# The sums of squares of the second half of x, taken up from the tenth projection step on instead of the fifth

## The chip, the core and the metric

The kernel runs on one core of one Trainium2 chip. The metric is the device time of one execution in microseconds, as the median of several runs. A core has TensorE (PE in the rows, its weight loads PEld), VectorE (DVE), ScalarE (ACT), GpSimd (POOL) and SyncE (SP), which here issues the DMAs. Each engine works through its own queue of instructions in the order in which the program wrote it, and waits at semaphores for the others.

## What is computed

One layer of a decoder: sliding-window attention with sinks, between a projection of the normalised input and a projection of the gated output. x has 2048 tokens of 2048 features, all in float32. There are 32 query heads and 4 key and value heads of 64 features each; a block of 128 queries sees its own and the block of keys before it.

```python
h = rms_norm(x, swa_norm)                        # mean of x*x over the features
q, k, v, gate = split(h @ w_in)                  # 2048, 256, 256, 2048 columns
q, k = rms_norm(q, q_gain), rms_norm(k, k_gain)  # by head
s = q @ k * 64 ** -0.5 + bias[distance]          # 128 queries x 256 keys, banded
m = max(max(s), sink)
p = exp(s - m) / (sum(exp(s - m)) + exp(sink - m))
out = x + ((p @ v) * silu(gate)) @ w_out
```

The part that the change touches is the mean of x*x over the features, of which there is one number for each token. It enters the key and query norms as a small correction (eps_t) and scales the values and gates (rstd).

## The kernel before

**Tiling.** The tokens are worked on in two halves of 1024 (HALF). For each half the transposed x lies in SBUF as 16 tiles, each split into a high and a low part (bigh, bigl), and a projection step takes 128 columns of w_in: three matmuls (L148, L151, L154) for each of the 16 tiles and of two column groups of 512 tokens, so 96 matmuls into the two accumulators acc. There are 40 such steps, numbered from 0: for each half and each of two pairs of key heads a step for the keys, one for the values and eight for the queries. Steps 0 to 9 and 10 to 19 are the two pairs of the first half, 20 to 29 and 30 to 39 those of the second.

**Attention units.** Beside the matmuls of step n the program emits attention units (beside, unit) whose queries are ready: four units for each query step, 128 in all, each with two blocks of queries and two heads. A unit has scores s (8 matmuls, L329; written 4 and 4 where it is the first block), a masking copy on VectorE (L333, L334, L337), the reading of the scores with scale and bias into lg (L342, 4 instructions), maximum and exponentials (L346 to L357), normalisation on GpSimd (L360), four transposes (pt, L364), copies and masks, eight output matmuls (o, L383; 6 for a first block), and a store. In PSUM there is one buffer each for s, pt and o; lg has two.

**The statistics.** For the first half the squares are summed while x is loaded. For the second half block_sums (L170) does it: for each of eight blocks of 128 tokens it loads four pieces of x in its untransposed form (xb, L174) and squares each on ScalarE with an accumulator (L175). Then stats(1) (L177) reduces the 32 columns to one number for each token, forms eps_t and rstd, and transposes rstd on PE (tp, L191) through the o buffer and an lg buffer (rr, L192, L193), writes it to DRAM (r_sp, L194) and reads it back as a row (rb, L198), which the gates use much later. The squares' buffers come from the pool evp (4 buffers), which the key and value work and the query squares use as well.

**The loop.** Lines 492 to 506 run over the steps from 3 on: load the next weights, block_sums of one block in steps 4 to 11, stats(1) in step 12, the units, the 96 matmuls, and the work on the result (evacuate). Ahead of step 20 the second half of x is loaded (load_big(1), L100 to L102). After the 40 steps come the gates and the output projection (from L507 on), 14 passes of 8 steps with 48 matmuls each.

**What sets the order.** The program is given to a scheduler, which simulates it and writes the instructions of every engine in the order in which its simulation could start them, by the order of emission as a priority; key work and the loading of x stand higher than their place. So an emission that moves changes the written order of every engine around it, and later, and the matmuls of units and projections interleave in another way.

Of the kernel before, what the change touches and what calls it, by code (L numbers as in the profile page):

```python
# [21 lines left out]
NB = HALF // P  # L22
# [9 lines left out]
def swa_layer_kernel(ctx: ExitStack, tc: tile.TileContext, xT: bass.AP, x: bass.AP, w_in: bass.AP,  # L32
# [60 lines left out]
    def load_big(c, ks=range(KT), cuts=(0, HALF), xsq=None):  # L93
        hi, lo = [], []
        for k in ks:
            raw = st.tile([P, HALF], F32, tag="raw", name="raw", bufs=RAW)
            h, l = [big.tile([P, HALF], F32R, tag="big", name=n) if k < KT - 2 else
                    rest.tile([P, HALF], F32R, tag="rest", name=n) for n in ("bigh", "bigl")]
            for a, b in zip(cuts, cuts[1:]):
                nc.sync.dma_start(out=raw[:, a:b], in_=xT[k * P:(k + 1) * P, c * HALF + a:c * HALF + b])  # L100
                nc.scalar.activation(out=h[:, a:b], in_=raw[:, a:b], func=AF.Copy, scale=gT[:, k:k + 1])  # L101
                nc.vector.scalar_tensor_tensor(out=l[:, a:b], in0=raw[:, a:b], scalar=gT[:, k:k + 1],  # L102
                                               in1=h[:, a:b].bitcast(F32), op0=ALU.mult, op1=ALU.subtract)
                if xsq:
                    square_sums(k, raw, a, b, xsq)
            hi.append(h)
            lo.append(l)
        return hi, lo


    def load_stat(src, qs=range(2), cuts=(0, HALF), between=None, eng=nc.vector):
        parts = []
        for q in qs:
            raw = st.tile([P, HALF], F32, tag="raw", name="raw", bufs=RAW)
            for a, b in zip(cuts, cuts[1:]):
                nc.sync.dma_start(out=raw[:, a:b].rearrange("p (k c) -> p k c", c=P),
                                  in_=src[:, q * 8 + a // P:q * 8 + b // P, :])
                if between and a == 0:
                    between()
            parts += split_stat(raw, cuts, eng)  # L120
        return parts
# [19 lines left out]
    def gemm(stat, res, acc=None, ks=range(KT), last=KT - 1):  # L141
        if acc is None:
            acc = new_acc()
        for k in ks:
            h, l = stat[k // 4]
            cs = slice((k % 4) * P, (k % 4 + 1) * P)
            for n in range(2):
                nc.tensor.matmul(acc[n], h[:, cs], res[0][k][:, n * CH:(n + 1) * CH],  # L148
                                 start=(k == 0), stop=False)
            for n in range(2):  # L150
                nc.tensor.matmul(acc[n], h[:, cs], res[1][k][:, n * CH:(n + 1) * CH],  # L151
                                 start=False, stop=False)
            for n in range(2):
                nc.tensor.matmul(acc[n], l[:, cs], res[0][k][:, n * CH:(n + 1) * CH],  # L154
                                 start=False, stop=(k == last))
        return acc
# [13 lines left out]
    def block_sums(b):  # L170

        for i in range(4):
            xs = evp.tile([P, CH], F32, tag="ev", name="xb")
            nc.sync.dma_start(out=xs, in_=x[b * P:(b + 1) * P, i * CH:(i + 1) * CH])  # L174
            nc.scalar.activation(out=xs, in_=xs, func=AF.Square, accum_out=msum[:, b % NB, i:i + 1])  # L175

    def stats(c, xsq=None):  # L177
        bs = slice(c * NB, (c + 1) * NB)
        ms = at.tile([P, NB], F32, tag="ms", name="ms")
        if xsq:  # L180
            ss = ps_t.tile([P, NB], F32, tag="t", name="xss")
            for b in range(NB):
                nc.tensor.matmul(ss[:, b:b + 1], xsq[b // 4][:, b % 4 * P:(b % 4 + 1) * P], ones, start=True, stop=True)
        else:
            ss = at.tile([P, NB], F32, tag="xss", name="xss", bufs=1)
            nc.vector.tensor_reduce(out=ss, in_=msum, op=ALU.add, axis=AX.X)
        nc.vector.tensor_scalar(out=ms, in0=ss, scalar1=1.0 / D, scalar2=EPS, op0=ALU.mult, op1=ALU.add)
        nc.vector.tensor_scalar(out=eps_t[:, bs], in0=ms, scalar1=EPS, scalar2=None, op0=ALU.mult)
        nc.gpsimd.tensor_tensor(out=rstd[:, bs], in0=ms, in1=mhalf[:, 0:NB], op=ALU.pow)
        tp = ps_o.tile([P, CH], F32, tag="o", name="tp")  # L190
        nc.tensor.transpose(out=tp[0:NB, 0:P], in_=rstd[:, bs], identity=ident)  # L191
        rr = at.tile([P, CH], F32, tag="lg", name="rr")  # L192
        nc.vector.tensor_copy(out=rr[0:NB, 0:P], in_=tp[0:NB, 0:P])  # L193
        nc.sync.dma_start(out=r_sp[c][:, :], in_=rr[0:NB, 0:P])  # L194
# [205 lines left out]
    def stat_src(step):  # L400
        kind, c, i = step
        return w_in[{"q": 0, "k": 16, "v": 18}[kind] + i]
# [7 lines left out]
    def evacuate(step, acc, copies=None):  # L410
        kind, c, i = step
        if kind == "q":
            queries[i, c] = evac_q(acc, c)
        elif kind == "k":
            with tc.high_priority(offset=400):
                evac_k(acc, c, i, copies or copy_out(acc))
        else:
            evac_v(acc, c, i, copies or copy_out(acc))
# [3 lines left out]
    def beside(n):  # L422

        for cb, j in units.get(n, []):
            c, half = j // NB, j % NB // 4
            if (cb, c) not in bias:
                bias[cb, c] = load_bias(cb)
            if (cb // 4, c, half) not in kv:
                kv[cb // 4, c, half] = load_kv(cb // 4, c, half)
            qs, rq = queries[cb, c]  # L430
            unit(cb, j, qs[half], rq, *kv[cb // 4, c, half], bias[cb, c])
# [60 lines left out]
    for n, step in enumerate(steps):  # L492
        if n < 3:
            continue
        nxt = load_stat(stat_src(steps[n + 1]), eng=nc.gpsimd) if n + 1 < len(steps) else None
        if 4 <= n < 4 + NB:
            block_sums(NB + n - 4)
        elif n == 4 + NB:
            stats(1)
        beside(n)  # L500
        acc = gemm(stat, res)
        if n + 1 < len(steps) and steps[n + 1][1] != step[1]:
            with tc.high_priority(offset=300):
                res = load_big(1)
        evacuate(step, acc)
        stat = nxt
# [269 lines left out]
```

## Time and profile before

| | |
|---|---|
| median of 3 runs | 2465.68 us (2463.45 to 2465.91) |
| the profiled execution | 2466.36 us |
| its span | 2464.6 us |
| mean granted clock of PE | 0.994 |
| PE busy | 2431.2 us, 99% of the span |
| VectorE, GpSimd, ScalarE busy | 67%, 44%, 39% |

The span is the time from the first to the last instruction, and the execution's own time lies 1.8 us above it. The profile is one execution. Its views that are used here: the busy time by engine; the busy time in stretches of 20 us with the granted clock as a share of the full 2.4 GHz; the table of who waited for whom; the chain of waits, which follows the end of the work back to what released each piece; the rows of one tile; and the timeline of an engine. Counted off in PE's projection matmuls in the trace, 96 to a step, step 8 lies at 210 to 251 us, steps 10 and 11 at 280 to 355, step 14 at 414 to 439, step 19 at 560 to 590, steps 20 and 21 at 590 to 666, and step 31 at 931 to 964.

### The profile page before, as it was taken

The numbers are of one execution on the slowest core, as the hardware profiler recorded it, in microseconds if no ns is written. First come the engines' busy times: TensorE is split into PE (matmuls) and PEld (weight loads), VectorE is DVE, ScalarE is ACT, GpSimd is POOL, SyncE is SP. The second block draws the span as 40 slices with busy tenths as digits, with TensorE's granted clock in tenths as the row PEclk, the third lists the DMA queues.
The fourth block names the chain that finished last, engine by engine and source line by source line (L and its number), as shares of the span: only waits on it lengthen the run. The fifth ranks groups of instructions, "written<-read, shape, count | busy, mean of one in ns | idle before, by whom it ended". The sixth has DMA issues, their size and how long they took to land.

```text
span 2464.6 us, 35291 instructions
## 1 busy us (share of the span) xinstructions
PE 2431.2 (99%) x11858; PEld 2044.4 (83%) x11858; DVE 1648.4 (67%) x3206; ACT 971.6 (39%) x2387; POOL 1092.3 (44%) x1041
## 2 busy tenths in 40 slices
PE   8999999999999999999999999999999999999999
PEld 7888888887788888888887888888888888888887
DVE  7287777789777877887864776576684436554533
ACT  7255545456545545554543332222232212122110
POOL 0156666575656666666541343034451033113434
PEclk9999999999999999999999999999999999999999
DMA  7322333125331223212127997687887679678755
GB/s 228 104 95 90 109 98 119 59 68 172 107 105 57 78 63 105 86 52 84 65 86 269 316 363 257 236 271 260 263 271 260 224 228 346 213 265 278 262 181 175
DMA packets 211380, 429.39 MB, mean 174 GB/s; under 512 B 20208, under 2 KB 91520, under 8 KB 211200
## 3 DMA queue, kind: packets, MB, share of 16 engines
q1 hardware_dynamic: 211200, 427.15, 53.1%
q8 instruction: 94, 1.54, 0.3%
q14 instruction: 86, 0.70, 0.1%
HBM read 336.88 MB, written 90.19 MB: 173 GB/s over the span
## 4 chain that ended last, share of the span: by engine, by line
PE 87%; DMA 7%; DVE 3%; POOL 1%; issue 1%; ACT 1%; SPq 0%; DVEq 0%; POOLq 0%; ACTq 0%
PE acc L148 25%; PE acc L151 25%; PE acc L154 25%; PE s L329 5%; PE o L383 5%; DMA braw<-xT 2%; PE pt L364 2%; DMA out<-craw 1%; DMA craw<-x 1%; DMA raw<-xT 1%; DVE parts L520 0%; DMA braw<-t_sp 0%; POOL craw L523 0%; DVE braw L520 0%; DVE braw L572 0%
## 5 line engine op out<-in xcount | busy, mean ns | idle before, releaser
L148 PE MATMUL acc<-bigh,wh 128*128 128x512 f32 x1472 | 494.4, 396 | 7.7 <-ACT bigh L101 5.5
L154 PE MATMUL acc<-bigh,wl 128*128 128x512 f32 x1472 | 491.1, 394 | 0.0
L151 PE MATMUL acc<-bigl,wh 128*128 128x512 f32 x1472 | 490.5, 395 | 0.1
L523 POOL TENSOR_TENSOR craw<-craw,u 128x512 f32<-128x512 f32 x112 | 163.0, 1469 | 419.7 <-DMA craw<-x 229.1
L148 PEld LDWEIGHTS acc<-bigh,wh 128*128 128x128 f32 x1472 | 274.3, 190 | 58.3 <-ACT bigh L101 5.5
L151 PEld LDWEIGHTS acc<-bigl,wh 128*128 128x128 f32 x1472 | 275.2, 190 | 51.9 <-DVE bigl L102 1.3
L154 PEld LDWEIGHTS acc<-bigh,wl 128*128 128x128 f32 x1472 | 274.5, 190 | 50.5
L355 ACT ACTIVATE lg<-lg,nm 128x128 f32<-128x128 f32 x512 | 199.9, 392 | 185.0 <-DVE nm L348 169.2
L151 PE MATMUL acc<-obl,parts 128*128 128x512 f32 x768 | 236.6, 389 | 1.4 <-DVE obl L520 1.4
L154 PE MATMUL acc<-obh,parts 128*128 128x512 f32 x768 | 236.6, 389 | 0.4 <-DVE parts L520 0.4
L154 PE MATMUL acc<-obh,wl 128*128 128x512 f32 x768 | 236.5, 389 | 0.0
L148 PE MATMUL acc<-obh,parts 128*128 128x512 f32 x768 | 236.4, 389 | 0.0
L148 PE MATMUL acc<-obh,wh 128*128 128x512 f32 x768 | 236.4, 389 | 0.0
L151 PE MATMUL acc<-obl,wh 128*128 128x512 f32 x768 | 236.4, 389 | 0.0
L134 POOL TENSOR_TENSOR wl<-raw,wh 128x512 fp32r<-128x512 f32 x144 | 187.5, 1303 | 94.7 <-ACT wh L133 87.9
L523 POOL TENSOR_TENSOR araw<-araw 128x1024 f32<-128x1024 f32 x48 | 119.6, 2492 | 225.5 <-DMA araw<-o_sp 75.3
L360 POOL TENSOR_TENSOR lg<-lg,den 128x512 f32<-128x512 f32 x128 | 134.1, 1048 | 112.1 <-DVE den L359 74.0
L563 ACT CAST obh<-braw 128x1024 fp32r<-128x1024 f32 x80 | 83.9, 1053 | 230.1 <-DVE braw L520 108.7
L151 PEld LDWEIGHTS acc<-obl,parts 128*128 128x128 f32 x768 | 143.9, 188 | 31.8 <-DVE obl L520 2.2
L154 PEld LDWEIGHTS acc<-obh,parts 128*128 128x128 f32 x768 | 144.2, 188 | 30.9 <-DVE parts L520 0.9
L151 PEld LDWEIGHTS acc<-obl,wh 128*128 128x128 f32 x768 | 144.2, 188 | 30.0
L148 PEld LDWEIGHTS acc<-obh,parts 128*128 128x128 f32 x768 | 144.1, 188 | 30.1
(136 smaller groups left out, 4405.8 us busy)
## 6 DMA issues: line engine op xcount, KB each, us to landing
braw<-w_out SPq DMA_DIRECT2D x88, 512.0 KB, 5.6
araw<-w_in SPq DMA_DIRECT2D x80, 512.0 KB, 5.7
araw<-o_sp SPq DMA_DIRECT2D x80, 512.0 KB, 5.7
raw<-w_in SPq DMA_DIRECT2D x79, 512.0 KB, 3.7
braw<-xT SPq DMA_DIRECT2D x72, 512.0 KB, 5.8
craw<-o_sp SPq DMA_DIRECT2D x80, 256.0 KB, 4.9
o_sp<-og SPq DMA_DIRECT2D x128, 128.0 KB, 1.9
o_sp<-craw SPq DMA_DIRECT2D x64, 256.0 KB, 5.0
```

Source lines behind the costliest of these rows:

```text
L134: eng.tensor_tensor(out=l[:, a:b], in0=r, in1=h[:, a:b].bitcast(F32), op=ALU.subtract)
L148: nc.tensor.matmul(acc[n], h[:, cs], res[0][k][:, n * CH:(n + 1) * CH], start=(k == 0), stop=False)
L151: nc.tensor.matmul(acc[n], h[:, cs], res[1][k][:, n * CH:(n + 1) * CH], start=False, stop=False)
L154: nc.tensor.matmul(acc[n], l[:, cs], res[0][k][:, n * CH:(n + 1) * CH], start=False, stop=(k == last))
L329: nc.tensor.matmul(s[:, b, h, lo:], qq[:, h, (i0 + b) * P:(i0 + b + 1) * P], kk[:, i, (i0 + b) * P + lo:(i0 + b + 2) * P], start=(i == 0), ...
L355: nc.scalar.activation(out=lg[:, b, h], in_=lg[:, b, h], func=AF.Exp, bias=nm[:, b, h:h + 1], accum_out=den[:, b, h:h + 1])
L360: nc.gpsimd.tensor_tensor(out=lf, in0=lf, in1=den.rearrange("p b h -> p (b h)").unsqueeze(2).broadcast_to([P, 4, P]), op=ALU.mult)
L364: nc.tensor.transpose(out=t[:, i, :], in_=lf[:, i, :], identity=ident)
L383: nc.tensor.matmul(o[:, 2 * b:2 * b + 2, :], v, p[:, 2 * b:2 * b + 2, :], start=(i == 0), stop=(i == len(terms) - 1))
L523: nc.gpsimd.tensor_tensor(out=out, in0=a, in1=b, op=op)
L563: nc.scalar.copy(out=h, in_=src)
```

## The change

The block sums move from steps 4 to 11 to steps 9 to 16, and stats(1) from step 12 to step 17. Each step still takes one block, in the same order of blocks.

```diff
@@ -493,9 +493,9 @@
         if n < 3:
             continue
         nxt = load_stat(stat_src(steps[n + 1]), eng=nc.gpsimd) if n + 1 < len(steps) else None
-        if 4 <= n < 4 + NB:
-            block_sums(NB + n - 4)
-        elif n == 4 + NB:
+        if 9 <= n < 9 + NB:
+            block_sums(n - 9 + NB)
+        elif n == 9 + NB:
             stats(1)
         beside(n)
         acc = gemm(stat, res)
```

What the scheduler makes of it, at three places. In these rows a name is a tile, and what stands behind the arrow is read. The names: acc are the projections, s the scores, pt the transposes, o the outputs of attention units.

PE's queue in step 8 before, from the second group of scores (a first block) on; ahead of these rows stand a score group, four transposes and six outputs.

```order
L329 MATMUL s<-kk,qq 128x256 x4
L364 MATMUL pt<-ident,lg 128x128 x4
L383 MATMUL o<-php,vv 128x256
L383 MATMUL o<-plp,vv 128x256
L383 MATMUL o<-ph,vv 128x256
L383 MATMUL o<-pl,vv 128x256
L383 MATMUL o<-php,vv 128x256
L383 MATMUL o<-plp,vv 128x256
L383 MATMUL o<-ph,vv 128x256
L383 MATMUL o<-pl,vv 128x256
L329 MATMUL s<-kk,qq 128x256 x8
L148 MATMUL acc<-bigh,wh 128x512
```

The same place after.

```order
L329 MATMUL s<-kk,qq 128x256 x4
L364 MATMUL pt<-ident,lg 128x128 x4
L383 MATMUL o<-php,vv 128x256
L383 MATMUL o<-plp,vv 128x256
L383 MATMUL o<-ph,vv 128x256
L383 MATMUL o<-pl,vv 128x256
L383 MATMUL o<-php,vv 128x256
L383 MATMUL o<-plp,vv 128x256
L383 MATMUL o<-ph,vv 128x256
L383 MATMUL o<-pl,vv 128x256
L148 MATMUL acc<-bigh,wh 128x512
L151 MATMUL acc<-bigl,wh 128x512
```

The third score group has moved away from behind the eight outputs; it now follows after 21 projection matmuls.

PE's queue in step 15 before, behind the row transpose tp. Between tp and these rows stand 23 projection matmuls.

```order
L148 MATMUL acc<-bigh,wh 128x512 x2
L151 MATMUL acc<-bigl,wh 128x512
L329 MATMUL s<-kk,qq 128x256 x8
L151 MATMUL acc<-bigl,wh 128x512
L154 MATMUL acc<-bigh,wl 128x512 x2
L148 MATMUL acc<-bigh,wh 128x512 x2
L151 MATMUL acc<-bigl,wh 128x512 x2
L154 MATMUL acc<-bigh,wl 128x512 x2
L148 MATMUL acc<-bigh,wh 128x512 x2
L151 MATMUL acc<-bigl,wh 128x512 x2
L154 MATMUL acc<-bigh,wl 128x512
L364 MATMUL pt<-ident,lg 128x128 x4
```

PE's queue after, behind tp, which now stands in step 19. Between tp and these rows stand 14 projection matmuls.

```order
L148 MATMUL acc<-bigh,wh 128x512
L151 MATMUL acc<-bigl,wh 128x512
L154 MATMUL acc<-bigh,wl 128x512
L329 MATMUL s<-kk,qq 128x256 x8
L364 MATMUL pt<-ident,lg 128x128 x4
L329 MATMUL s<-kk,qq 128x128 x4
L329 MATMUL s<-kk,qq 128x256 x4
L383 MATMUL o<-php,vv 128x256
L148 MATMUL acc<-bigh,wh 128x512
L151 MATMUL acc<-bigl,wh 128x512
```

From tp to the first transposes pt it was 40 projection matmuls and a score group, and is 17 and a score group; a second score group follows those transposes at once.

SyncE's queue around the write of the transposed row before: w_in are weights, og outputs of units.

```order
L390 DMA o_sp_102<-og 128x256
L116 DMA raw<-w_in 128x1024
L194 DMA r_sp_152<-rr 8x128
L198 DMA rb_15243<-r_sp_152 128x1024
L116 DMA raw<-w_in 128x1024
L390 DMA o_sp_103<-og 128x256
L305 DMA bias<-band 128x256
L116 DMA raw<-w_in 128x1024
```

SyncE's queue there after: xT is the second half of x, kk and vv are keys and values.

```order
L100 DMA raw<-xT 128x1024
L316 DMA vv<-v_sp_94 128x4x128
L390 DMA o_sp_106<-og 128x256
L194 DMA r_sp_152<-rr 8x128
L198 DMA rb_15243<-r_sp_152 128x1024
L315 DMA kk<-k_sp_90 128x2x640
L305 DMA bias<-band 128x256
L100 DMA raw<-xT 128x1024 x2
L390 DMA o_sp_106<-og 128x256
L100 DMA raw<-xT 128x1024 x5
```

The write (L194) and the read (L198) stood among loads of weights, and now stand behind the first of the 16 loads of x and ahead of the other 15.

PE's queue in step 31 before, around the transposes of the second pair's keys (L247).

```order
L148 MATMUL acc<-bigh,wh 128x512
L151 MATMUL acc<-bigl,wh 128x512
L154 MATMUL acc<-bigh,wl 128x512
L247 MATMUL acc<-ident,kv 128x128 x8
L148 MATMUL acc<-bigh,wh 128x512
L151 MATMUL acc<-bigl,wh 128x512
L154 MATMUL acc<-bigh,wl 128x512
L148 MATMUL acc<-bigh,wh 128x512
L151 MATMUL acc<-bigl,wh 128x512
L154 MATMUL acc<-bigh,wl 128x512
L148 MATMUL acc<-bigh,wh 128x512
L364 MATMUL pt<-ident,lg 128x128
```

PE's queue in step 31 after, some way ahead of those transposes. A score group, four transposes and eight outputs stand just ahead of these rows.

```order
L329 MATMUL s<-kk,qq 128x256 x8
L364 MATMUL pt<-ident,lg 128x128 x4
L383 MATMUL o<-php,vv 128x256
L383 MATMUL o<-plp,vv 128x256
L383 MATMUL o<-ph,vv 128x256
L383 MATMUL o<-pl,vv 128x256
L383 MATMUL o<-php,vv 128x256
L383 MATMUL o<-plp,vv 128x256
L383 MATMUL o<-ph,vv 128x256
L383 MATMUL o<-pl,vv 128x256
L329 MATMUL s<-kk,qq 128x256 x8
L148 MATMUL acc<-bigh,wh 128x512
```

Three score groups now stand with only transposes and outputs between them, where before projection matmuls stood. In steps 10 and 11 PE's queue has the same rows before and after, and ScalarE's squares stand in the same places.

## Rows read from the trace of the kernel before

**Rows 1.** The page's busy time of each engine, us (share of the span) xinstructions.

```profile
PE 2431.2 (99%) x11858; PEld 2044.4 (83%) x11858; DVE 1648.4 (67%) x3206; ACT 971.6 (39%) x2387; POOL 1092.3 (44%) x1041
```

**Rows 2.** Stretches: length, busy PE, PEld, DVE, ACT, POOL, clock, DMA share, GB/s.

```profile
220.00:240.00 20.00, 16.52 (x86) 14.16 (x85) 17.08 (x50) 12.76 (x44) 10.65 (x14) 0.83 0.34 106
...
280.00:300.00 20.00, 18.17 (x101) 15.79 (x100) 17.08 (x46) 10.97 (x37) 9.94 (x16) 0.91 0.23 71
...
320.00:340.00 20.00, 18.67 (x102) 15.66 (x101) 16.72 (x42) 13.45 (x45) 10.45 (x15) 1.00 0.26 83
340.00:360.00 20.00, 18.30 (x98) 15.70 (x97) 14.84 (x40) 9.19 (x31) 15.30 (x13) 0.91 0.35 98
...
420.00:440.00 20.00, 20.00 (x94) 16.60 (x93) 8.83 (x28) 5.05 (x15) 9.31 (x9) 1.00 0.27 87
...
580.00:600.00 20.00, 18.40 (x90) 14.09 (x90) 18.84 (x31) 13.59 (x26) 11.22 (x10) 1.00 0.68 202
600.00:620.00 20.00, 17.52 (x85) 14.22 (x84) 19.66 (x39) 12.69 (x23) 10.36 (x10) 0.92 0.60 196
620.00:640.00 20.00, 17.84 (x98) 15.29 (x97) 16.92 (x42) 11.25 (x38) 13.14 (x16) 0.99 0.32 107
640.00:660.00 20.00, 20.00 (x102) 16.89 (x102) 15.48 (x47) 10.72 (x38) 13.57 (x12) 0.91 0.17 47
660.00:680.00 20.00, 18.12 (x107) 15.29 (x106) 12.10 (x32) 9.79 (x26) 12.01 (x16) 1.00 0.66 171
...
960.00:980.00 20.00, 20.00 (x121) 17.75 (x120) 15.24 (x41) 12.53 (x41) 13.04 (x17) 1.00 0.73 204
```

**Rows 3.** PE's waits, 100 to 700 us: us in total, times, longest.

```profile
PE s L329 <- DVE lg L342: 5.8, 5, 2.2
PE pt L364 <- DVE pl L368: 2.7, 3, 1.9
PE o L383 <- POOL plp L372: 1.9, 3, 1.3
```

**Rows 4.** The tile xb of the squares: duration ns min/median/max, first and last start.

```profile
L174 SPq DMA_DIRECT2D xb<-x x32: 328/336/1438, 126.6 to 368.3; - x32
L175 ACT ACTIVATE xb<-xb x32: 614/631/638, 130.4 to 376.0; 128x512 f32<-128x512 f32 x32
L175 ACT ACTIVATION_READ_ACCUMULATOR xb<-xb x32: 184/188/197, 131.0 to 376.5; 128x1 f32 x32
```

**Rows 5.** The chain of waits, 205 to 235 us: start us, us, what.

```profile
220.96 0.95 PE s L329 x8
...
222.34 0.72 PE o L383 x6
...
229.33 1.14 DVE lg L342 x4
...
230.60 2.04 PE s L329 x8
```

**Rows 6.** Timeline of DVE and POOL behind the row transpose: start us, us, instruction.

```profile
435.07 0.28 DVE L193 COPY rr<-tp 8x128 f32<-8x128 f32 x1 [4.52 <-PE tp L191]
435.28 1.10 DVE L342 SCALAR_TENSOR_TENSOR lg<-s,rq,bias 128x128 f32<-128x128 f32 x4
...
439.64 1.04 POOL L360 TENSOR_TENSOR lg<-lg,den 128x512 f32<-128x512 f32 x1 [4.67 <-ACT wh L133]
```

**Rows 7.** Timeline of PE at the row transpose.

```profile
434.76 0.27 PE L191 MATMUL tp<-ident,rstd 128*8 128x128 f32 x1
...
435.10 0.63 PE L151 MATMUL acc<-bigl,wh 128*128 128x512 f32 x2
435.57 0.61 PE L154 MATMUL acc<-bigh,wl 128*128 128x512 f32 x2
```

**Rows 8.** Timeline of SyncE's queue there: issue us, us.

```profile
435.42 0.29 SPq L194 DMA_DIRECT2D r_sp<-rr  x1
438.73 0.34 SPq L198 DMA_DIRECT2D rb<-r_sp  x1
```

## The prediction

> **What bounds the kernel now.** I read the page's busy line first [rows 1]: TensorE (PE) is busy for 2431.2 of 2464.6 us. So only what makes PE stand, or run at a lower clock, can move the time; what other engines do counts where PE waits for it. Next come the 20 us stretches of the first 1320 us [rows 2]. I use one measure throughout: the loss of a stretch is 20 us less PE's busy time, plus 20 us times what the granted clock lacks to 1.00 (part of such a stretch ran at the 1.2 GHz level in place of 2.4). Four of the stretches shown lie in the first half of x: 220:240 loses 3.48 + 3.4 = 6.9 us, 280:300 1.83 + 1.8 = 3.6, 320:340 1.3, 340:360 1.7 + 1.8 = 3.5; together 15.3. Five lie around the loading of the second half, 580 to 680: 1.6 + 4.1 + 2.4 + 1.8 + 1.9 = 11.7. The stretches 420:440 and 960:980 lose nothing; they hold the row transpose of the statistics and the key and value steps of the second half's second pair.
>
> What is waited for there: the table of PE's waits from 100 to 700 us has as its largest row scores (s, L329) behind the reading of the scores before them (lg, L342), 5.8 us in 5 waits [rows 3]. There is one buffer of scores, so the scores of a unit can't start before VectorE has read those of the unit ahead. Where projection matmuls (acc) stand between two score groups, that costs nothing. The chain of waits through 220 to 232 us shows the other case [rows 5]: scores at 220.96, outputs (o) to 223.06, then six or seven microseconds in which ScalarE and VectorE lead the chain, the reading of scores at 229.33, the next scores at 230.60. PE follows its written order, so the projections queued behind do not fill this. I call such a place, with score groups separated only by transposes and outputs of other units, a knot.
>
> The sums of squares themselves: 32 loads, issued from 126.6 to 368.3 us, and 32 squares with 32 accumulator reads on ScalarE, 0.631 + 0.188 = 0.82 us each, 26.2 us in all [rows 4]. They are on PE's path nowhere directly: no row of PE's waits names them among its largest.
>
> **The change part by part.** *The sums.* Nothing is removed or added: the same 32 loads, 32 squares, one reduction, one transpose, two small DMAs. The 26.2 us of ScalarE go from steps 5 to 12 into steps 10 to 17. By themselves I cost this at nothing: what hides it is ScalarE's idle time, since it is busy for 39% of the span [rows 1]. Where a square delays an exponential or a cast on PE's path it costs up to 0.82 us; in steps 10 and 11, where PE's order stays, ScalarE has squares in the same places before and after. What the move does is make the scheduler place everything else differently, and there the sum lies.
>
> *Step 8's knot.* Before, three score groups stand with only transposes and outputs between; now the third has 21 projection matmuls ahead of it. What is left is the pattern that stands in step 10, before and after alike, and step 10 loses 3.6 us (280:300). So 6.9 becomes 3.6: a gain of **3.3 us**; bounds 0 (the loss is of the remaining pair) and 6.9 (all goes).
>
> *Steps 10 and 11.* PE's order is the same row for row, so 3.6 + 1.3 + 3.5 us stay: 0.
>
> *Step 31's new knot.* Here the new order has three score groups in a row, with 4 transposes and 8 outputs between each, ahead of the transposes of the second pair's keys. The old order had projections there and 960:980 lost nothing. The nearest row is step 8's old knot, 6.9 us: the same three groups with the same transposes, outputs and query casts between, and no square beside them that I would have to take off. The bounds are 0 (VectorE is less busy here) and 8 (that knot with a wait more). I take **+6.9 us**.
>
> *The row transpose of the statistics (tp, L191).* It moves from step 14 to step 19. The pass behind it is measured: transpose at 434.76, copy (L193) at 435.07, reading of the next scores at 435.28, normalised exponentials (L360) at 439.64 + 1.04 = 440.68 us [rows 6, 7]; so 5.9 us from transpose to the next unit's transposes. Before, 40 projection matmuls and a score group cover that. Now 17 projections at 0.23 us (two take 0.47 from start to start [rows 7]) and one score group of 0.95 [rows 5] cover 3.9 + 0.95 = 4.9: a wait of 1.0 us. Behind it the next scores come at once, and wait for a masking copy, a query cast and the reading (0.7 + 0.7 + 1.1 us by the same kind of rows; of these only the reading, 1.14, is in rows 5): I take 1.2 us. The first output then waits some 0.4 us. That is **+2.6 us**; bounds 0, and 4.3 with one fall of the clock as in 280:300 or 340:360 (1.8).
>
> *Steps 20 to 22.* The units that stood still around the transpose are caught up here. Now there are three places where a score group follows the one before with 1.1 to 1.4 us of PE work between; before there was one, with 0.6. But the VectorE work between the query casts of step 17 and the key work of step 20 is the same in both orders (12 units and the 16 loads of x), and this stage was held by VectorE and the loads. I keep 11.7 us, so **0**; bounds -3 (the loads stand closer together) and +8 (two of the places at step 10's 3.6, and a little).
>
> Sum: -3.3 + 0 + 6.9 + 2.6 + 0 = +6.2 us. The profiled execution took 2466.36 us with a span of 2464.6; the median is 2465.68, so the profile stands for the runs within 0.7 us, and I add the sum to the median: 2465.7 + 6.2 = **2471.9 us**, 0.25% slower. A measurement of this kernel can tell about 0.2% (4.9 us) from no change.
>
> **The rivals.** *No change that can be measured.* Step 31's knot costs half or less (3 us), since VectorE there has no x to take up: -3.3 + 3 + 2.6 = +2.3, 2468 us. For it: 960:980 lost nothing. Against: no three groups stood in a row there.
>
> *Faster.* The mechanism is step 8: 6.9 us go entirely if it was the squares on ScalarE, four of them in a row of that knot, that held the query casts and through them VectorE; then step 31, without squares, costs nothing, and 2465.7 - 6.9 = 2458.8, or 2461.4 with the transpose's 2.6. It decides at the point where a knot without squares costs under 1 us. Against it: in ScalarE's order the squares stand behind the exponentials of the knot's first two units, and 280:300 lost 3.6. The Trainium skill, Perfetto Trace Analysis, Optimization Strategy, says that a gap that repeats on the engine that should be saturated can mean too few buffers for the next tile; by that the single score buffer sets the loss and squares do not, the largest row of PE's waits agrees, and a gain by the squares would not come.
>
> *The loads of x held up, slower still.* On the queue of SyncE the write of r_sp and the read of rb now stand ahead of 15 of the 16 loads of the second half of x; before, they stood among loads of weights. In the trace the read went 3.31 us after the write was issued (435.42 to 438.73) [rows 8], and nothing was issued between. If this falls where the loads are what PE waits for, 3.3 us more and a fall of the clock (1.8) come on top: 2471.9 + 5.1 = 2477 us. Against it: step 19 now begins with 36 projections with hardly anything between, which frees the old x sooner. The Trainium skill, DMA: Bandwidth & Descriptors, Anatomy of one DMA, says that a wait for a semaphore happens on the issuing sequencer before dispatch; by that the wait for the landed row keeps all loads behind it back, and the trace agrees in the 3.31 us, which is this rival's price.
>
> That the sums come too late for their reader, the second half's first keys, is excluded: the reduction stands at step 17 and VectorE has it ahead of those keys in either order.
>
> **How the numbers follow.** The forecast has a chance of 0.38, the held loads 0.12, no change 0.33, faster 0.17. Slower by over 0.2% (above 2470.6): 0.38 + 0.12 = 0.50; within: 0.33; faster (below 2460.8): 0.17. The range reaches from 2460, a little under the faster case with the transpose's cost, to 2482, the held loads with the upper bound of one further place (+5); below and above I leave 0.1 each.
>
> **What would show it.** In the profile after, the stretch around 220 us should lose about 3.6 us, that around 285 and 345 as before; a new loss of 6 to 7 us should stand near 930 to 950, with scores behind the reading of scores as PE's waits; a loss of 2 to 4 near 565; 580 to 680 about 12. I am wrong if 900 to 960 stays without loss, or if 580 to 680 loses under 8 or over 17 us: then the stage of the loads, which I put at zero, decided.

## The result and the profile after

The changed kernel takes 2486.83 us (median of 5 runs, 2484.04 to 2494.16), the kernel before beside it 2464.41 us: a ratio of 1.0094, with an interval of 1.0077 to 1.011. It is slower, as forecast, but by 22 us and not by 6, and outside the range. The profiled execution took 2486.83 us too, with a span of 2485.1.

The page's busy line of the changed kernel answers [rows 1]: the instructions of every engine are as many as before, so the 20.5 us of span are waits and clock. PE's busy time rose by 6.0 us with the same 11858 matmuls, with a granted clock of 0.91 in 560 to 680 us in place of 0.97; the other 14.5 us are PE standing.

```profile
PE 2437.2 (98%) x11858; PEld 2045.3 (82%) x11858; DVE 1649.0 (66%) x3206; ACT 973.5 (39%) x2387; POOL 1098.6 (44%) x1041
```

The stretches of the changed kernel answer [rows 2], with the same columns (length; busy PE, PEld, DVE, ACT, POOL; clock, DMA share, GB/s).

```profile
220.00:240.00 20.00, 18.18 (x100) 15.59 (x99) 17.63 (x47) 10.48 (x34) 11.46 (x14) 0.91 0.25 80
...
280.00:300.00 20.00, 17.78 (x104) 15.24 (x103) 16.95 (x45) 11.97 (x41) 10.80 (x17) 1.00 0.30 96
...
320.00:340.00 20.00, 18.65 (x112) 15.96 (x111) 17.79 (x50) 14.78 (x47) 10.83 (x12) 1.00 0.34 100
340.00:360.00 20.00, 18.24 (x97) 15.36 (x96) 11.81 (x29) 8.13 (x26) 15.11 (x17) 1.00 0.49 126
...
540.00:560.00 20.00, 20.00 (x99) 16.78 (x98) 2.98 (x7) 3.63 (x6) 8.33 (x11) 1.00 0.26 85
560.00:580.00 20.00, 17.91 (x95) 14.95 (x94) 16.57 (x40) 8.02 (x25) 7.10 (x8) 1.00 0.34 95
580.00:600.00 20.00, 15.40 (x68) 12.02 (x68) 18.09 (x35) 15.19 (x33) 12.62 (x10) 0.83 0.48 163
600.00:620.00 20.00, 15.85 (x68) 11.71 (x69) 19.79 (x31) 13.04 (x22) 9.62 (x10) 0.83 0.70 226
...
940.00:960.00 20.00, 17.11 (x98) 14.14 (x97) 14.34 (x38) 9.66 (x33) 9.65 (x16) 1.00 0.08 27
```

By the prediction's measure of loss, and from rows like these, the difference between 200 and 2440 us is made up so:

| us from the start | loss before | loss after | difference |
|---|---|---|---|
| 200 to 280 | 6.7 | 3.9 | -2.8 |
| 280 to 360 | 8.1 | 5.3 | -2.8 |
| 360 to 540 | 0.1 | 2.4 | +2.3 |
| 560 to 680 | 11.7 | 26.6 | +14.9 |
| 900 to 1000 | 0.0 | 4.1 | +4.1 |
| 1360 to 1460 | 0.4 | 4.8 | +4.4 |
| all other | 8.5 | 7.3 | -1.2 |

The sum is +18.9; the other 1.6 us of the 20.5 lie below what this measure sees. Most of the unexpected time stands in 560 to 680, where the second half of x is loaded. These two rows show that stretch as one, before and then after, and are the yardstick for the experiments (loss: 120 - 111.89 + 3.6 = 11.7, and 120 - 104.23 + 10.8 = 26.6).

```profile
560.00:680.00 120.00, 111.89 (x584) 92.85 (x583) 101.32 (x230) 70.19 (x177) 74.78 (x76) 0.97 0.46 139
```

```profile
560.00:680.00 120.00, 104.23 (x519) 85.81 (x518) 104.94 (x236) 69.20 (x181) 69.87 (x68) 0.91 0.40 128
```

**What the trace shows there.** The row of 540 to 560 is the odd one: VectorE is busy for 2.98 of 20 us, right ahead of the stage of the loads, in which it is busy for 18 to 20 of 20 us from 580 to 640. Its timeline in the changed kernel shows three waits in a row, the last of them for the row transpose (in brackets: idle before, and what ended it).

```profile
547.28 0.69 DVE L368 TENSOR_TENSOR pl<-pt,ph 128x512 fp32r<-128x512 f32 x1 [6.55 <-ACT ph L366]
547.89 0.84 DVE L389 TENSOR_TENSOR og<-o,bot 64x256 f32<-64x256 f32 x2
555.56 0.85 DVE L389 TENSOR_TENSOR og<-o,bot 64x256 f32<-64x256 f32 x2 [6.83 <-ACT bot L386]
560.93 0.28 DVE L193 COPY rr<-tp 8x128 f32<-8x128 f32 x1 [4.52 <-PE tp L191]
561.14 1.10 DVE L342 SCALAR_TENSOR_TENSOR lg<-s,rq,bias 128x128 f32<-128x128 f32 x4
```

PE lost nothing meanwhile: it ran projections. What it left out are attention units, which stand behind the transpose. VectorE's reading of scores ahead of the copy began at 530.22, so it takes up no new unit for 30 us. The next reading stands right behind the row's copy in VectorE's queue, and starts ahead of the row's write (561.24): what holds it is this place in the written order, and not the write. In the table of VectorE's waits in the kernel before, the same last wait stood ahead of step 14's transpose, with the same 4.5 us: there too VectorE stood half idle, 8.83 of 20 us in the row 420:440 of [rows 2]. So the hole in VectorE's work was there before. What is new is where it lies.

Behind it, the chain of waits of the changed kernel (start, us, what) runs through VectorE and the loads, PE hardly appearing: readings of scores and query casts of the late units stand between the low parts of x (bigl), and the low parts release the buffer of the next load.

```profile
589.00 0.69 DVE qq L214
...
589.72 1.13 DVE lg L342 x4
...
592.04 1.27 DVE bigl L102
...
593.32 3.73 DMA raw<-xT
...
597.08 1.07 ACT bigh L101
...
599.16 0.60 DVE lg L342 x2
599.76 0.73 DVE bigl L102
```

The waits of SyncE's queue, 500 to 700 us, give the same from the side of the loads (us in total, times, longest): before, then after.

```profile
SPq L100 <- DVE bigl L102: 16.8, 9, 3.4
```

```profile
SPq L100 <- DVE bigl L102: 29.1, 11, 7.5
```

### The profile page after: what moved, and what is told of

It reads as the page before. It is cut to its first block, busy times and chain, and to the rows that moved or that the text cites. A ratio compares the mean times of both kernels' runs of the same rounds, so it can differ in the third digit from the quotient of the medians.

```text
span 2485.1 us, 35274 instructions
## 1 busy us (share of the span) xinstructions
PE 2437.2 (98%) x11858; PEld 2045.3 (82%) x11858; DVE 1649.0 (66%) x3206; ACT 973.5 (39%) x2387; POOL 1098.6 (44%) x1041
## 4 chain that ended last, share of the span: by engine, by line
PE 86%; DVE 5%; DMA 4%; ACT 2%; issue 1%; POOL 1%; SPq 0%; DVEq 0%; ACTq 0%; POOLq 0%
PE acc L148 25%; PE acc L151 25%; PE acc L154 25%; PE s L329 4%; PE o L383 4%; DMA braw<-xT 2%; PE pt L364 2%; DVE lg L342 1%; DMA o_sp<-craw 0%; DMA braw<-t_sp 0%; DVE bigl L102 0%; ACT lg L355 0%; DMA xb<-x 0%; ACT ph L366 0%; DVE qq L214 0%
## 5 line engine op out<-in xcount | busy, mean ns | idle before, releaser
L151 PE MATMUL acc<-bigl,wh 128*128 128x512 f32 x1472 | 498.3, 395 | 0.2 <-DVE bigl L102 0.2
L154 PE MATMUL acc<-bigh,wl 128*128 128x512 f32 x1472 | 496.3, 395 | 0.0
L342 DVE SCALAR_TENSOR_TENSOR lg<-s,rq,bias 128x128 f32<-128x128 f32 x512 | 144.0, 343 | 60.6 <-PE pt L364 52.5
L360 POOL TENSOR_TENSOR lg<-lg,den 128x512 f32<-128x512 f32 x128 | 135.5, 1058 | 96.8 <-DVE den L359 69.6
```

Source lines behind the costliest of these rows:

```text
L342: nc.vector.scalar_tensor_tensor(out=lg[:, b, h], in0=s[:, b, h, P:], scalar=r, in1=bt[:, h, :], op0=ALU.mult, op1=ALU.add)
L360: nc.gpsimd.tensor_tensor(out=lf, in0=lf, in1=den.rearrange("p b h -> p (b h)").unsqueeze(2).broadcast_to([P, 4, P]), op=ALU.mult)
```

## The experiments

The theory formed on this trace, the **hole**: the row transpose takes the only buffer of o and one of the two of lg. The units behind it stand behind its copy in the written order, PE runs on with projections, VectorE stands idle for some 17 us, and beside the loads of x, where VectorE sets the pace, this is not made up. The rivals: the squares in their new steps; SyncE's queue with the write and read of the row ahead of the loads; an unlucky interleaving of units and loads, whatever the transpose does. Times are given with the ratio to the kernel before, run beside each, and its interval. The runs are called e1 to e12, as marked.

**e1, moving the statistics alone** (sums in steps 4 to 11, as before):

```diff
-        elif n == 4 + NB:
+        elif n == 9 + NB:
             stats(1)
```

> The block sums stay in steps 4 to 11 as before; stats(1) alone moves, from step 12 to step 17. Theory of the hole: the row transpose takes the o buffer and an lg buffer, the units stand still for some 20 us just ahead of the loading of x, and VectorE's idle time there (17 us in 540 to 560 of the changed kernel) has to be caught up while the loads fill VectorE: then 560 to 680 us loses 20 to 28 us here too, and the time is 2478 to 2490. Rival, the squares: it is the squares beside steps 10 to 17 that cost, by ScalarE or by the evp buffers: then the time is within 5 us of before (2464).

Measured: 2484.9 us, 1.0076 (1.006 to 1.0091). VectorE is busy for 4.83 of 20 us in 540 to 560, and 560 to 680 loses 26.3. The move of stats(1) makes nearly all of the change's cost (1.0076 of 1.0094); that of the squares makes little of it.

**e2, the changed kernel with the row's copy in a buffer of its own:**

```diff
-        rr = at.tile([P, CH], F32, tag="lg", name="rr")
+        rr = at.tile([P, P], F32, tag="rr", name="rr", bufs=1)
```

> The changed kernel, with the copy of the transposed row (rr) in a buffer of its own instead of one of the two lg buffers; sums in steps 9 to 16, stats(1) in step 17, write and read of the row where they were. Theory of the hole, by the lg buffer: no stretch ahead of the loading in which VectorE is under half busy, 560 to 680 loses about 12 us as before, time 2464 to 2474. Rival, the squares: no change from the changed kernel, 2482 to 2490. Rival, SyncE's queue (write and read of the row ahead of the loads of x): no change from it either.

Measured: 2471.61 us, 1.0026 (1.0014 to 1.0038). Its rows of 540 to 560 and 560 to 680:

```profile
540.00:560.00 20.00, 20.00 (x110) 17.35 (x110) 16.31 (x44) 9.80 (x29) 12.65 (x15) 1.00 0.37 119
560.00:680.00 120.00, 109.40 (x569) 90.32 (x568) 100.53 (x219) 69.37 (x179) 72.95 (x77) 0.96 0.42 131
```

VectorE's hole is gone (its readings of scores around the copy start 7.5 us apart, at 561.34 and 568.80) and the loss falls from 26.6 to 15.4. The write and the read of the row still stand ahead of 15 loads in SyncE's queue, at 564.01 and 567.48, so that rival doesn't make the 14.9 us. The 3.7 us that this stage still loses more than in the kernel before are within its price, but e8 below, with the row written long behind the loads, loses as much.

**e3, the changed kernel without the transpose,** rstd written to r_sp number by number:

```diff
+        if c:
+            nc.sync.dma_start(out=r_sp[c].rearrange("b p -> p b"), in_=rstd[:, bs])
+            return
         tp = ps_o.tile([P, CH], F32, tag="o", name="tp")
```

> The changed kernel, with rstd of the second half written to the row's place in DRAM by one DMA of single numbers, without the transpose on PE, its copy, and the o and lg buffers. Theory of the hole: the units do not stand still at all, 560 to 680 loses 12 us or less, time 2460 to 2472. The squares or SyncE's queue as the cause: 2482 to 2490, since both stay.

Measured: 2469.84 us, 1.001 (0.9997 to 1.0023); 560 to 680 loses 12.4, 900 to 1000 nothing. With the transpose away, the change costs nothing that can be told from no change. Two limits: the profiled execution (2464.71) is the quickest of its ten, and the read of the row stands at 501.53 here, 53 us ahead of the first load, so that SyncE's queue did not stay as it was, though the expectation took it to.

**e4, the changed kernel without the sums of squares:**

```diff
+    nc.gpsimd.memset(msum, 64.0)
...
         if 9 <= n < 9 + NB:
-            block_sums(n - 9 + NB)
+            pass
```

> The changed kernel without the loads and squares of the block sums: the sums are a constant, so the second half's mean squares are not those of x; stats(1) stays in step 17. Theory of the hole: the transpose still stops the units ahead of the loading, 560 to 680 loses 20 to 28 us, time 2476 to 2490. Rival, the squares: the loss of the change goes away, time within 5 us of before or under it (2458 to 2469).

Measured: 2476.96 us, 1.0044 (1.0029 to 1.0059). In all it is 10 us quicker than the changed kernel (12 by the ratios), but 560 to 680 loses 27.0. The squares are not what this stretch pays for; what leaving them out gives lies elsewhere (360 to 540 and 900 to 1000 lose nothing and 1360 to 1460 1.6, while 280 to 360 loses 8.7).

**e5, the kernel before without the transpose** (the edit of e3 in the kernel before):

> The kernel before, sums and stats(1) where they were, with the second half's rstd written to DRAM by one DMA of single numbers in place of the transpose, copy and o and lg buffers. Theory of the hole: before, the units stand still in step 14 as well, but there are five steps without a load behind it, so the hole there costs next to nothing: 2458 to 2468. If a hole costs its length wherever it stands, this gains 10 us or more: under 2456.

Measured: 2477.16 us, 1.0045 (1.003 to 1.006): a miss. The stage of the loads is as before (13.2), but PE has one new wait at 390, in the table of its waits from 360 to 540 us:

```profile
PE o L386 <- DVE og L392: 8.5, 1, 8.5
```

SyncE's queue there (issue, us) shows why: the reader of the row (L201) waits for the write of single numbers (L191), issued 10.5 us ahead of it, and holds back the store of a unit (L393) that VectorE's buffer og needs.

```profile
379.50 0.44 SPq L191 DMA_DIRECT2D r_sp<-rstd  x1
380.04 0.61 SPq L116 DMA_DIRECT2D raw<-w_in  x1
389.97 0.33 SPq L201 DMA_DIRECT2D rb<-r_sp  x1
390.40 0.38 SPq L393 DMA_DIRECT2D o_sp<-og  x1
```

So the prediction's third rival is a real mechanism, with another price and in another place: 10 us of a held queue, when a store that the units need stands behind it. In e3 the same wait (491.43 to 501.53 us) fell where nothing was missing.

**e6, sums in steps 7 to 14, statistics at step 15** (against the kernel before):

```diff
-        if 4 <= n < 4 + NB:
-            block_sums(NB + n - 4)
-        elif n == 4 + NB:
+        if 7 <= n < 7 + NB:
+            block_sums(NB + n - 7)
+        elif n == 7 + NB:
```

> Sums in steps 7 to 14, stats(1) in step 15: the row transpose comes in step 16 to 17 of PE's order, three steps ahead of the load. Theory of the hole: the units have caught up in part, 560 to 680 loses 12 to 18 us, time 2464 to 2474. If squares beside steps 10 to 14 cost, or a late arrival of the statistics, the time lies between, 2474 to 2482.

Measured: 2482.03 us, 1.0069 (1.005 to 1.0088): a miss, and the useful one. The hole now lies two steps earlier, at 460 to 500, and 540 to 560 has none; yet 560 to 680 loses 27.4. The theory, that a hole costs only where it touches the stage of the loads, falls.

```profile
460.00:480.00 20.00, 20.00 (x104) 17.02 (x103) 7.01 (x13) 5.89 (x10) 11.59 (x15) 1.00 0.21 66
480.00:500.00 20.00, 20.00 (x100) 16.73 (x99) 9.38 (x25) 8.04 (x26) 5.58 (x6) 1.00 0.22 70
...
560.00:680.00 120.00, 104.61 (x515) 86.39 (x514) 103.15 (x230) 68.58 (x175) 71.78 (x76) 0.90 0.36 118
```

**e7, the kernel before with a second row transpose,** the same row transposed, copied and written once more at step 17 (`row` is the last part of `stats`, from the tile tp on, made a function that `stats` calls too; all else as before):

```diff
+        if n == 9 + NB:
+            row(1)
```

> The kernel before, with the transpose of the row, its copy and its write done a second time in step 17 (the same numbers again); sums, eps_t and rstd as before. Nothing of the change is done but the stop of the units by the second transpose. Theory of the hole: the units stand still ahead of the load once more, VectorE is under half busy in 540 to 560 us, 560 to 680 loses 18 to 28 us, time 2472 to 2488. If the squares or the lateness of the statistics were the cause: 2462 to 2468.

Measured: 2482.61 us, 1.0064 (1.0044 to 1.0083). The transpose in that place with its copy, write and read, and with the sums and their reduction left where they were, costs what the change costs there. (The write and the read stand ahead of the loads here too, at 565.18 and 566.49; e2 is what tells them from the transpose.)

```profile
540.00:560.00 20.00, 20.00 (x104) 17.01 (x103) 5.61 (x14) 5.84 (x16) 11.65 (x15) 1.00 0.15 49
560.00:680.00 120.00, 105.61 (x523) 87.45 (x523) 106.58 (x239) 70.44 (x187) 71.88 (x68) 0.90 0.40 128
```

**e8, the changed kernel with the row transposed only at step 24** (the same call `row(1)` at `n == 24`, and no transpose in stats(1)):

> The changed kernel with sums in steps 9 to 16 and eps_t and rstd in step 17, but the transpose of the row in step 24, where nothing is loaded beside the units. Theory of the hole: the hole moves to some 760 to 790 us, costs nothing there, 560 to 680 loses 12 to 14 us; time 2460 to 2472. If the hole costs wherever it stands: 2478 or more.

Measured: 2469.07 us, 1.0013 (1.0 to 1.0025); 560 to 680 loses 16.5, more than the 12 to 14 expected; the time is within its range. The hole is now at 740 to 760 us, and PE is busy all through it and the 60 us behind it:

```profile
740.00:760.00 20.00, 20.00 (x93) 16.54 (x93) 6.19 (x16) 5.80 (x16) 7.62 (x8) 1.00 0.18 66
```

**The second theory, the carry.** To hold both e6 and the rest I counted, in PE's written order, how many units' scores stand ahead of the first projection of step 19 (eight score matmuls a unit). A hole anywhere makes PE run ahead of the units, since it does projections in their place. By this theory nothing is lost if the units are taken up again before step 19; those that are not are added to VectorE's work beside the loads. The kernel before has its hole at step 14 and then four units in each of the steps 15 to 18, and 49 ahead of step 19; the changed kernel has 47. This count is known before a kernel runs. The last four runs were priced by its counterpart, the units whose scores stand in steps 19 to 22.

**e9, e6 with the row's own buffer** (the edit of e2): 50 units ahead of step 19, where e6 has 47.

> The sums in steps 7 to 14 and the statistics at step 15, as in the kernel of the sums from step 7 on, but with the row's copy (rr) in a buffer of its own in place of one of the two of lg. That kernel had 16 units' scores standing in PE's order in steps 19 to 22 (12.25 in the kernel before) because the units held up behind the transpose in step 16 were not caught up ahead of step 19, and lost 27.5 us in 560 to 680. With the row's own buffer PE's order holds no gap of more than 0.55 steps between score groups there, and 12.25 scores in steps 19 to 22. Theory of the carry (what the transpose holds up and is not done when step 19 begins is added to VectorE's work in steps 19 to 22): 560 to 680 loses 11 to 16 us, time 2460 to 2470. Rival (the loads and units of that kernel were merely interleaved badly, whatever the transpose did): over 22 us lost in 560 to 680, time 2476 or more.

Measured: 2458.62 us (2456.18 to 2458.95), 0.9965 (0.9951 to 0.9979). The stage of the loads loses 4.3 us, less than the theory's own 11 to 16, so the time came out below its range as well; 27.4 became 4.3 by one buffer, and the order that came with it. This kernel is quicker than both the kernel before and the changed one.

```profile
460.00:480.00 20.00, 20.00 (x115) 17.37 (x114) 15.66 (x38) 11.52 (x36) 13.88 (x19) 1.00 0.16 53
480.00:500.00 20.00, 20.00 (x109) 17.20 (x108) 15.02 (x45) 6.98 (x24) 12.79 (x14) 1.00 0.27 85
...
560.00:680.00 120.00, 116.87 (x630) 99.80 (x629) 104.80 (x237) 75.98 (x196) 80.11 (x85) 0.99 0.51 158
```

**e10, sums in steps 5 to 12, statistics at step 13** (the form of e6 with 5 in place of 7): 46 units.

> The sums in steps 5 to 12, the statistics at step 13: the smallest move. The gap between score groups in PE's order then lies at steps 13.7 to 15.3 as in the kernel before (13.7 to 15.1), but only 12.4 scores follow in steps 15 to 18 (15.2 before), and 15 stand in steps 19 to 22 (12.25 before). Theory of the carry: some 2.75 units more for VectorE beside the loads, at about 7 us of VectorE each some 19 us, of which a part is hidden: 560 to 680 loses 20 to 27 us, time 2472 to 2482. Rival (only a gap right ahead of step 19 costs, one at step 14 is caught up): 560 to 680 loses 10 to 14, time 2460 to 2468.

Measured: 2492.88 us, 1.011 (1.0087 to 1.0133): the slowest of all, by a move of one step, with the hole where the kernel before has it. 560 to 680 loses 27.1, the upper end of what the carry gave; the time is 11 us above its range, which had counted this stage alone: 360 to 540 loses 2.8 and 1360 to 1460 6.1 us more than in the kernel before, and the profiled execution is among the quickest of its four (2488.07 to 2501.13).

```profile
420.00:440.00 20.00, 20.00 (x97) 16.62 (x96) 6.99 (x22) 4.20 (x7) 9.87 (x9) 1.00 0.27 83
...
560.00:680.00 120.00, 103.73 (x507) 83.64 (x506) 99.09 (x226) 67.13 (x173) 70.45 (x72) 0.91 0.38 123
```

**e11, sums in steps 6 to 13, statistics at step 14** (with 6): 46 units too.

> The sums in steps 6 to 13, the statistics at step 14: gap at steps 14.4 to 15.75, 10.4 scores in steps 15 to 18, 14 in steps 19 to 22 (12.25 before). Theory of the carry: 560 to 680 loses between the kernel before (11.8) and that from step 7 on (27.5), 16 to 24, time 2468 to 2479. Rival (a gap there is caught up): 10 to 14, time 2460 to 2468.

Measured: 2485.62 us, 1.0077 (1.0063 to 1.0091); 560 to 680 loses 20.9, within the carry's 16 to 24 and far from the rival's 10 to 14. The time is 7 us above its range, which had again counted this stage alone: 360 to 540, 900 to 1000 and 1360 to 1460 lose 2.6, 4.2 and 2.8 us more than in the kernel before.

**e12, the kernel before with the row's own buffer** (the edit of e2): 49 units, no hole.

> The kernel before with the row's copy (rr) in a buffer of its own. No gap of more than 0.55 steps stands between score groups in PE's order in steps 13 to 30 (1.4 in the kernel before, at step 14), and 12.25 scores stand in steps 19 to 22, as before. Theory of the carry: the kernel before had caught up by step 19, so little is gained: 560 to 680 loses 10 to 14, time 2460 to 2467. Rival (every gap costs some time somewhere, also the one at step 14): 5 us or more faster, under 2459.

Measured: 2464.97 us, 0.9994 (0.9985 to 1.0002); 560 to 680 loses 9.3. So the hole that the kernel before had at step 14 was worth at most the 2.4 us between 11.7 and 9.3. That the whole time stays equal is two things together: 1360 to 1460 loses 4.6 us more here (5.1 against 0.4), for a reason that no run shows.

All together, by the count of units ahead of step 19:

| units | loss of 560 to 680, us |
|---|---|
| 50 | 4.3 (e9) |
| 49 | 9.3 (e12), 11.7 (before), 12.4 (e3), 15.4 (e2), 16.5 (e8) |
| 48 | 13.2 (e5) |
| 47 | 26.3 (e1), 26.4 (e7), 26.6 (after), 27.0 (e4), 27.4 (e6) |
| 46 | 20.9 (e11), 27.1 (e10) |

The other count, in the traces, of the units whose scores start in steps 19 to 22: 13 in e9, e12 and the kernel before (4.3 to 11.7 us lost), 14 in e3, e5, e2 and e8 (12.4 to 16.5) and in the changed kernel (26.6), 15 in e11, e1, e7 and e4 (20.9 to 27.0), 16 in e10 (27.1), 17 in e6 (27.4). Only the changed kernel stands out of this order.

From the first projection of step 19 to that of step 23, counted off in the traces, VectorE is busy for 107.6 of 125.8 us in e9, 111.0 of 135.7 in the kernel before, 118.2 of 148.3 in the changed one, 125.9 of 159.7 in e10 and 132.2 of 160.7 in e6. So more work of VectorE goes with longer steps, but isn't all of it: it stands for 18 us of them in e9 and for 25 to 34 in the other four.

What these runs don't show: the count was never changed by itself, only through the buffer, the transpose and the steps, which reorder all else. The count ahead of step 19 parts the kernels with 48 to 50 units from those with 46 and 47, but within one count the losses differ by up to 7 us (9.3 to 16.5 at 49), as much as one unit seems to be worth between e9 and the kernel before. That the missing units are what costs is therefore argued; that the row's transpose and copy ahead of the loads cost is shown by e7, e3, e2 and e8 together. Why the order of e10 doesn't catch up, with its hole where the kernel before has it, is open.

## Why the prediction was off, step by step

*The sums in their new steps*: forecast 0. In the eight kernels in which the squares moved (the changed one, e2, e3, e6, e8 to e11), 360 to 540 loses 2.4 to 3.1 us, most of it in 380 to 420; in the kernel before, e1, e7 and e12, where they stay, and in e4, which has none, at most 0.4 (e5 has its held queue there). So the move of the squares goes with some 2.3 us in this stretch, a term put at nothing. Whether by ScalarE itself or by the order is not shown.

*Step 8's knot*: forecast 6.9 to 3.6 in the stretch of 220; measured 20 - 18.18 + 1.8 = 3.6. Right. The squares were not what held it: the changed kernel has none in this step and still loses 3.6, and e6 and e11, with four squares at 229 to 235 us, lose 3.3 in 200 to 280, against 3.9 in the changed kernel. So the rival *faster*, which needed a knot without squares to cost under 1 us, falls.

*Steps 10 and 11*: forecast 0; measured -2.8. The stalls are the same (1.83 became 2.22, 1.33 became 1.35, 1.70 became 1.76), but the granted clock, 0.91 in 280:300 and 340:360 of [rows 2], stays at 1.00. A small gain that the prediction had no term for.

*Step 31's knot*: forecast +6.9 (0 to 8), measured +4.1 in 900 to 1000, of which 2.9 stand in 940:960. The place was right, the term mis-sized: the knot costs less than step 8's, without a fall of the clock (1.00 against 0.83 in step 8's stretch [rows 2]). VectorE is busy for 14.34 of 20 us there, against 17.08; that this is the reason is not shown. PE's waits in 920 to 980 are many and short, the longest 0.9 us for the normalisation (L360); of the wait that the prediction named, scores behind the reading of scores, there are 0.3 us. In 1360 to 1460, in the gates' stage, 4.4 us more are lost, with the DMA engines' share at 0.96 (0.97 before). Over all kernels this loss went from 0.0 (e5) to 6.6 us (e1); no run was made on it, and it stays open.

*The row transpose itself*: forecast +2.6, made of a wait of 1.0 for the next transposes and 1.2 for the next scores. In PE's timeline after, these two are

```profile
566.59 0.66 PE L364 MATMUL pt<-ident,lg 128*128 128x128 f32 x4 [0.88 <-POOL lg L360]
568.42 0.80 PE L329 MATMUL s<-kk,qq 128*128 128x128 f32 x5 [1.17 <-issue]
```

and 560:580 loses 20 - 17.91 = 2.1. Right, as far as it went.

*Steps 20 to 22*: forecast 0 (-3 to +8). This is the step that failed; by the prediction's own sign, over 17 us in 580 to 680, this stage decided, for it loses 24. Of the 14.9 us of 560 to 680 12.8 are left when the 2.1 are taken off, beyond the upper bound. The prediction wrote that "the units that stood still around the transpose are caught up here", and put this at nothing because VectorE's work between two marks, step 17's casts and step 20's key work, is equal in both orders. Equal work was true; but the engine that does it stood idle between the marks for some 17 us, and in this stage VectorE is busy for 18 to 20 of 20 us from 580 to 640, which leaves it little room to catch up. The marks hid it: ahead of step 19 stand 49 units before and 47 after. It priced what PE waits for behind the transpose, and not what VectorE doesn't do meanwhile. The row that would have told was among those read: 420:440 of [rows 2], with PE at 20.00 and VectorE at 8.83. It was taken as a stretch that loses nothing. It does lose nothing itself; that it cost little later either (e12) goes with the 16 units that the kernel before takes up in steps 15 to 18, where e10, with the same hole and 13 units in those steps, loses 27.1 in 560 to 680.

The Trainium skill, Perfetto Trace Analysis, Optimization Strategy, says that a kernel can have several regimes in which the most contended engine changes, and that interleaving regimes can help. The runs go that way, in both directions: the units ahead of step 19 are work for VectorE out of the regime in which it has room, and those behind it are work in the one in which it has none. One unit more ahead of it than before (e9) goes with 7.4 us less lost, two units less with some 15 us more, three with 9 and 15; kernels with the same 49 units differ by 7.

*The rivals.* SyncE held by the row's write and read: in the changed kernel the read follows the write by 1.2 us (561.24 to 562.45), not 3.31, and e2, where it follows by 3.5 us with 15 loads behind it, loses 15.4 and not 26.6; not the cause, though e5 shows the mechanism at 10 us. No change, and faster: not so.

## What to carry to other kernels

Where the pace passes from one engine to another for a while, as here from PE to VectorE beside the loads, ask for every moved instruction what the engine of the next stage leaves undone until then: count, in the new order, how much of its work stands ahead of that stage. A small user of a ring buffer (here one transpose of 8 rows in the buffers of o and lg) stopped all the units that share the ring, and the cost came up later, where there was little room to make it up. A buffer of its own for the copy took the stop away in all three orders in which it was tried (e2, e9, e12). Alone it gave nothing (e12), and with the sums moved by three steps it gave 0.35% (e9).

## What was not expected of the hardware

A write of 1024 single numbers from 128 partitions held its reader, and with it SyncE's queue, for 10 us (379.50 to 389.97 in e5, 491.43 to 501.53 in e3), where the transposed row, written as 8 rows of 128, held it for 1.2 us in the changed kernel, 3.3 in the kernel before and 3.5 in e2. And stalls of about the same sum did not always go with a fall of the granted clock: 280:300 ran at 0.91 with 1.83 us of stalls in the kernel before and at 1.00 with 2.22 in the changed one, 340:360 at 0.91 with 1.70 and at 1.00 with 1.76.
